# Weight sums of the first six matrices between the products of the matrix before, down sums one matrix later

## The chip, the core and the metric

One core of a Trainium2 chip runs the whole kernel. The metric is the device time of one execution in microseconds (us), lower being better. The engines named below are TensorE (PE in the profile, PEld for its weight loads), VectorE (DVE), ScalarE (ACT), GpSimd (POOL) and SyncE (SP), which issues nearly all DMAs here; each runs its own instructions in order and waits for the others by semaphores.

## What is computed

One layer of a hybrid encoder on 1024 tokens of width 1024 in float32: a half feed-forward block, a token mixer, a second half feed-forward block, each between two RMS norms with a shift, scale and gate worked out from a condition vector.

```python
def swiglu(u, w_gate, w_up, w_down):
    return (jax.nn.silu(u @ w_gate) * (u @ w_up)) @ w_down

def sublayer(h, i, fn, resid_w):
    shift, scale, gate = mod[:, i, 0, None, :], mod[:, i, 1, None, :], mod[:, i, 2, None, :]
    u = rms_norm(h, norm_pre[l, i]) * (1.0 + scale) + shift
    return h + resid_w * gate * rms_norm(fn(u), norm_post[l, i])

h = sublayer(h, 0, lambda u: swiglu(u, ffn1_w_gate[l], ffn1_w_up[l], ffn1_w_down[l]), 0.5)
h = sublayer(h, 1, lambda u: token_mixer(u, ...), 1.0)
h = sublayer(h, 2, lambda u: swiglu(u, ffn2_w_gate[l], ffn2_w_up[l], ffn2_w_down[l]), 0.5)
```

The hidden width of a feed-forward block is 2816. The change lies in the gate and up products of the two blocks; the mixer between them is not touched.

## The kernel before

**Arithmetic.** Every product of the feed-forward blocks is a 2x2 block product with seven block products in place of eight (a Strassen form), and every float32 operand is held as a high and a low half, so that one block product is 4 blocks x 3 matmuls = 12 matmuls of 128x512 (`product`, L291 to L299). The activations' block sums (T1 to T4, B22) are made once for each feed-forward block. The weights' block sums are made for each matrix: S1, S2, S3, S4.

**Matrices and pairs.** A chunk pair c (11 of them, `NPAIR`) has two matrices, gate and up; the names m0, m1 (pair 0), m2, m3 (pair 1), m4, m5 (pair 2) and so on are used below. A matrix is `start` (two products with A11 and A12), then `p6` (S2 x T2), `p5` (S1 x T1), `p7` (S3 x T3), `p3` (S4 x B22), `p4` (A22 x T4). For the first three pairs (`NFIRST`) all six `start`s run ahead, while the activations' second half is still being prepared; their raw weights are given up by then, and are loaded again for the sums (`again`).

**The steps that the change moves.** `sums` (L319) loads the four raw blocks of a matrix as two transfers of 512 KB, r1 (tag "raw", two buffers) and r2 (tag "raw2", two buffers), makes S2 and S1 with two VectorE operations (L330, L331) in a tile s21, casts that on ScalarE (L224) and subtracts on VectorE (L225) to get the halves, and makes S3 and S4 with two more VectorE operations (L334, L335) in a tile s34. `sums34` (L337) makes the halves of those, `last` (L341) the halves of A22, which are read from r2. `hidden` (L437) takes the four results of a finished pair, makes their block sums with four VectorE operations in two tiles, and stores five tiles to DRAM. `down_sums` (L462) loads the four raw blocks of one chunk of the down weights (tags "raw" and "raw2"), makes four sums on VectorE in two tiles (t21, t34) and stores these. The sum tiles of `sums`, `hidden` and `down_sums` all have the tag "s" with four buffers. `steps` is a generator that loads one 512 KB row block of the condition weights (wada) at a time and adds it up on VectorE (L89, L91).

**Order.** The kernel is written as a program in one order; a planner lays it out on the engines, taking of what is ready by its own reckoning the operation that stands first in the program. An operation later in the program can therefore run ahead of one that waits, but buffers of one tag are handed out in program order. In the program of before, m2's sums stand behind all of pair 0, its `hidden` and its `down_sums`; m4's sums stand behind all of pair 1 and its `hidden`:

```python
if c == 0:
    rest(late, mats[c], True)
else:
    for second, m in enumerate(mats[c] if c < NFIRST else pair(c)):
        if second:
            down_sums(fp, late, A[wd][c], c, hd)
        m.start()
        rest(late, [m], c < NFIRST)
hidden(late, c, mats[c][1].c, hd)
```

Of the kernel before, what the change touches and what calls it, by code (L numbers as in the profile page):

```python
# [33 lines left out]
NPAIR = NFF // 2  # L34
ROWS = 4
QT = 13
NFIRST = 3
# [9 lines left out]
def build(ctx, tc, A, out):  # L47
# [253 lines left out]
    class Matrix:  # L301
# [80 lines left out]
        def start(self):  # L382
            self.part(4)
# [27 lines left out]
        H, L = TB[n]  # L411
        return lambda k: (H[k], L[k])

    def rest(late, ms, again):

        if len(ms) == 2:
            for m in ms:
                m.p6()
            for m in ms:
                m.p5()  # L420
                m.p3()
                m.p7()
            for m in ms:
                m.last()
                m.p4()
            return
        m = ms[0]
        m.sums(late, again)
        m.sums34()
        m.last()  # L430
        m.p6()
        m.p5()
        m.p7()
        m.p3()
        m.p4()

    def hidden(late, c, hs, hd):  # L437


        a11, a12, a21, a22 = hs["C11"], hs["C21"], hs["C12"], hs["C22"]  # L440
        s21 = late.tile([P, 2, HALF], F32, name="s21", tag="s", bufs=4)
        s34 = late.tile([P, 2, HALF], F32, name="s34", tag="s", bufs=4)
        V.tensor_add(s21[:, 1], a21, a22)
        V.tensor_sub(s21[:, 0], s21[:, 1], a11)
        V.tensor_sub(s34[:, 0], a11, a21)
        V.tensor_sub(s34[:, 1], a12, s21[:, 0])
        for n, t in (("A11", a11), ("A12", a12), ("A22", a22)):
            hd[n, c] = dram.tile([P, HALF], F32, name=f"hd_{n}_{c}_{len(hd)}")
            store_queue(c).dma_start(hd[n, c], t)
        both(hd, "S2", "S1", c, s21)  # L450
        both(hd, "S3", "S4", c, s34)

    def store_queue(c):

        return POOL if c == NPAIR - 1 else SP

    def both(hd, n0, n1, c, t):
        d = dram.tile([P, 2, HALF], F32, name=f"d_{n0}_{c}")
        hd[n0, c], hd[n1, c] = d[:, 0], d[:, 1]
        store_queue(c).dma_start(d, t)  # L460

    def down_sums(fp, late, src, c, hd):  # L462

        r1 = wpool.tile([P, 2, HALF], F32, name="raw", tag="raw", bufs=2)
        SP.dma_start(r1, src[:, 0:2])
        r2 = fp.tile([P, 2, HALF], F32, name="raw2", tag="raw2", bufs=2)
        SP.dma_start(r2, src[:, 2:4])
        t21 = late.tile([P, 2, HALF], F32, name="t21", tag="s", bufs=4)
        t34 = late.tile([P, 2, HALF], F32, name="t34", tag="s", bufs=4)
        V.tensor_sub(t21[:, 1], r1[:, 1], r1[:, 0])  # L470
        V.tensor_sub(t21[:, 0], r2[:, 1], t21[:, 1])
        V.tensor_sub(t34[:, 0], r2[:, 1], r1[:, 1])
        V.tensor_sub(t34[:, 1], r2[:, 0], t21[:, 0])
        both(hd, "T2", "T1", c, t21)
        both(hd, "T3", "T4", c, t34)

    def ffn(wg, wu, wd, start, pending, steps_fn, per_pair, steps2_fn, i, res_src, dst):


        hd = {}  # L480

        with tc.tile_pool(name="ffa", bufs=1, side="left", reuse_waits="tile") as fp, \
                tc.tile_pool(name="ffa_ps", bufs=1, space=PSUM, reuse_waits="tile") as psum:
            mats = {}

            def pair(c):
                g = Matrix(fp, psum, A[wg][c], None)
                mats[c] = g, Matrix(fp, psum, A[wu][c], g)
                return mats[c]

            first = [m for c in range(NFIRST) for m in pair(c)]
            start(fp, psum, first)
            with tc.tile_pool(name="fft", bufs=1, side="left", reuse_waits="tile") as tp, ExitStack() as more:
                pools = [tp]
                later = pending(pools, fp, psum, tag="y")
                for n, m in enumerate(first):
                    m.start()
                    if n:
                        next(later)
                with tc.tile_pool(name="ffs", bufs=1, side="left", reuse_waits="tile") as sp:  # L500
                    for m in first[:2]:
                        m.sums(sp, True, "s0")
                    for m in first[:2]:
                        m.sums34()
                pools.append(more.enter_context(tc.tile_pool(name="fft2", bufs=1, side="left", reuse_waits="tile")))
                for _ in later:
                    pass
                yp.close()
                mod_tag[0] = "pa"
                with tc.tile_pool(name="late", bufs=1, side="right", reuse_waits="tile") as late:  # L510
                    steps = steps_fn(late, psum)
                    for c in range(NPAIR):
                        if c == 0:
                            rest(late, mats[c], True)
                        else:
                            for second, m in enumerate(mats[c] if c < NFIRST else pair(c)):
                                if second:
                                    down_sums(fp, late, A[wd][c], c, hd)
                                m.start()
                                rest(late, [m], c < NFIRST)  # L520
                        hidden(late, c, mats[c][1].c, hd)
                        if c == 0:
                            down_sums(fp, late, A[wd][c], c, hd)
                            continue
                        for _ in range(per_pair):
                            next(steps, None)
                    for _ in steps:
                        pass
# [3 lines left out]
        with tc.tile_pool(name="ffb0", bufs=1, side="left", reuse_waits="tile") as np_, \  # L532
# [4 lines left out]
            steps = steps2_fn(np_, psum)  # L537
# [171 lines left out]
    def no_steps(fp, psum):  # L709
        yield  # L710

    pending = ffn("wg1", "wu1", "wd1", start0, pending0, steps1, 3, steps1b, 0, lambda t: A["x"][t * P:(t + 1) * P, :], lambda t: h_dram[0][t])

    pending = mixer(locals())

    ffn("wg2", "wu2", "wd2", start_half, pending, lambda fp, psum: mod_gate(fp, psum, 2, 0.5), 1, no_steps, 2, lambda t: h_dram[1][t],
        lambda t: out[t * P:(t + 1) * P, :])
    yp.close()
# [581 lines left out]
```

## Time and profile before

| | us |
|---|---|
| runs (three), median | 2326.1 |
| lowest, highest | 2325.53, 2331.6 |
| the profiled execution, its own time | 2332.79 |
| its span from first to last instruction | 2331.0 |
| mean granted TensorE clock, share of full | 0.975 |

| engine | busy us | share of the span |
|---|---|---|
| TensorE matmuls | 2204.7 | 95% |
| VectorE | 1570.6 | 67% |
| ScalarE | 1047.5 | 45% |
| GpSimd | 70.0 | 3% |

The page's busy shares are means over stages with different limits, so they only say which engine to look at; where it waits is read from the timeline of that engine, and what ends its waits from the timelines of the engines that it waits for. A row of a timeline gives the start, the duration, the engine, the line, what is written and read, and in brackets the idle time of the engine before it with what ended it.

### The profile page before, as it was taken

The numbers are of one execution on the slowest core, as the hardware profiler recorded it, in microseconds if no ns is written. First come the engines' busy times: TensorE is split into PE (matmuls) and PEld (weight loads), VectorE is DVE, ScalarE is ACT, GpSimd is POOL, SyncE is SP. The second block draws the span as 40 slices with busy tenths as digits, with TensorE's granted clock in tenths as the row PEclk, the third lists the DMA queues.
The fourth block names the chain that finished last, engine by engine and source line by source line (L and its number), as shares of the span: only waits on it lengthen the run. The fifth ranks groups of instructions, "written<-read, shape, count | busy, mean of one in ns | idle before, by whom it ended". The sixth has DMA issues, their size and how long they took to land.

```text
span 2331.0 us, 28613 instructions
## 1 busy us (share of the span) xinstructions
PE 2204.7 (95%) x10420; PEld 1805.3 (77%) x10420; DVE 1570.6 (67%) x2612; ACT 1047.5 (45%) x1882; POOL 70.0 (3%) x90
## 2 busy tenths in 40 slices
PE   5989999989989989999999999999979999999998
PEld 3767788868868877878888888788767787877876
DVE  6885787566667587576677677665976666655565
ACT  4523333335445465454554455555723332325454
POOL 1000000000000010011001000000000000000000
PEclk8899999999999999999999999999989999999999
DMA  7283574358877211110111122764465443427667
GB/s 298 75 286 131 202 259 175 137 181 304 299 234 237 69 45 40 41 47 29 60 55 64 46 86 87 244 199 128 140 244 179 143 169 138 173 96 261 201 203 246
DMA packets 137678, 364.39 MB, mean 156 GB/s; under 512 B 16704, under 2 KB 20800, under 8 KB 137536
## 3 DMA queue, kind: packets, MB, share of 16 engines
q1 hardware_dynamic: 135904, 356.79, 45.0%
q0 software_dynamic: 1632, 5.77, 0.6%
q8 instruction: 81, 1.33, 0.2%
q14 instruction: 61, 0.50, 0.1%
HBM read 272.32 MB, written 90.18 MB: 156 GB/s over the span
## 4 chain that ended last, share of the span: by engine, by line
PE 67%; DVE 17%; DMA 8%; ACT 4%; issue 3%; SPq 0%; DVEq 0%; ACTq 0%
PE bank L299 9%; PE bank L297 9%; PE bank L298 9%; PE pps L765 4%; PE pps L763 4%; PE pps L767 4%; DMA stg<-in_wd 3%; DVE f L960 2%; PE bankA L547 2%; PE bankA L549 2%; PE bankA L548 2%; DMA stg<-d_T 2%; PE bankB L547 2%; PE bankB L548 2%; PE bankB L549 2%
## 5 line engine op out<-in xcount | busy, mean ns | idle before, releaser
L763 PE MATMUL pps<-uH,wsH 128*128 128x512 f32 x512 | 209.7, 410 | 0.0
L765 PE MATMUL pps<-uL,wsH 128*128 128x512 f32 x512 | 205.4, 401 | 0.0
L767 PE MATMUL pps<-uH,wsL 128*128 128x512 f32 x512 | 204.7, 400 | 0.0
L225 DVE TENSOR_TENSOR tbL<-stg,tbH 128x512 fp32r<-128x512 f32 x154 | 105.8, 689 | 113.7 <-ACT tbH L224 113.4
L224 ACT CAST tbH<-stg 128x512 fp32r<-128x512 f32 x154 | 95.6, 621 | 167.8 <-DMA stg<-d_T 98.6
L547 PE MATMUL bankA<-tbH,sbH 128*128 128x512 f32 x352 | 140.8, 402 | 18.3 <-ACT tbH L224 17.9
L297 PE MATMUL bank<-uH,wsH 128*128 128x512 f32 x352 | 141.4, 404 | 3.5 <-DVE uH L179 2.7
L298 PE MATMUL bank<-uL,wsH 128*128 128x512 f32 x352 | 140.3, 398 | 1.5 <-POOL uL L180 1.5
L548 PE MATMUL bankA<-tbL,sbH 128*128 128x512 f32 x352 | 140.4, 399 | 0.0
L549 PE MATMUL bankA<-tbH,sbL 128*128 128x512 f32 x352 | 139.6, 397 | 0.0
L299 PE MATMUL bank<-uH,wsL 128*128 128x512 f32 x352 | 139.2, 396 | 0.0
L224 ACT CAST wsH<-s 128x1024 fp32r<-128x1024 f32 x88 | 91.6, 1049 | 97.1 <-DVE s L331 88.0
L141 DVE TENSOR_TENSOR wsL<-raw,wsH 128x1024 fp32r<-128x1024 f32 x72 | 87.9, 1221 | 69.1 <-ACT wsH L140 67.5
L225 DVE TENSOR_TENSOR sbL<-stg,sbH 128x512 fp32r<-128x512 f32 (+1 forms) x176 | 108.8, 620 | 36.3 <-ACT sbH L224 34.6
L224 ACT CAST sbH<-stg 128x512 fp32r<-128x512 f32 (+1 forms) x176 | 98.9, 565 | 70.8 <-DMA stg<-hd_A 40.7
L364 ACT COPY q<-bank 128x512 f32<-128x512 f32 x44 | 25.8, 587 | 209.2 <-PE bank L299 209.2
L547 PE MATMUL bankB<-tbH,sbH 128*128 128x512 f32 x264 | 104.5, 396 | 11.3 <-ACT y L599 10.9
L767 PEld LDWEIGHTS pps<-uH,wsL 128*128 128x128 f32 x512 | 96.9, 189 | 17.9
L763 PEld LDWEIGHTS pps<-uH,wsH 128*128 128x128 f32 x512 | 97.6, 191 | 14.7
L225 DVE TENSOR_TENSOR wsL<-s,wsH 128x1024 fp32r<-128x1024 f32 x88 | 106.9, 1218 | 2.6 <-ACT wsH L224 2.0
L765 PEld LDWEIGHTS pps<-uL,wsH 128*128 128x128 f32 x512 | 97.2, 190 | 14.7
L548 PE MATMUL bankB<-tbL,sbH 128*128 128x512 f32 x264 | 104.2, 395 | 0.0
(247 smaller groups left out, 5947.7 us busy)
## 6 DMA issues: line engine op xcount, KB each, us to landing
wada<-in_wada SPq DMA_DIRECT2D x56, 512.0 KB, 5.6
raw<-in_wg SPq DMA_DIRECT2D x50, 512.0 KB, 6.7
raw<-in_wu SPq DMA_DIRECT2D x50, 512.0 KB, 4.4
raw<-in_wd SPq DMA_DIRECT2D x44, 512.0 KB, 4.5
stg<-hd_A SPq DMA_DIRECT2D x88, 256.0 KB, 4.3
stg<-d_S SPq DMA_DIRECT2D x88, 256.0 KB, 3.1
stg<-d_T SPq DMA_DIRECT2D x88, 256.0 KB, 3.5
d_S<-s SPq DMA_DIRECT2D x40, 512.0 KB, 2.7
```

Of the source, the lines that this page charges most:

```text
L141: eng.tensor_sub(l, raw, h.bitcast(F32))
L224: ACT.copy(h, src)
L225: V.tensor_sub(l, src, h.bitcast(F32))
L297: PE.matmul(ps, H[:, ks], bH, start=first and k == 0, stop=False, skip_group_check=not first)
L298: PE.matmul(ps, H[:, ks], bL, start=False, stop=False, skip_group_check=not first)
L299: PE.matmul(ps, L[:, ks], bH, start=False, stop=k == 3, skip_group_check=not first)
L547: PE.matmul(ps, sH[:, ts], tH, start=first, stop=False, skip_group_check=not check)
L548: PE.matmul(ps, sH[:, ts], tL, start=False, stop=False, skip_group_check=not check)
L549: PE.matmul(ps, sL[:, ts], tH, start=False, stop=last, skip_group_check=not check)
L763: PE.matmul(ps, aH, bH, start=i == 0, stop=False)
L765: PE.matmul(ps, aH, bL, start=False, stop=False)
L767: PE.matmul(ps, aL, bH, start=False, stop=i == n - 1)
```

## The change

The order of the program alone changes, for pairs 0, 1 and 2 of each of the two feed-forward blocks. The same loads, sums, casts, products and stores are made. A new function `rest_first` walks the six first matrices. The sums of m2 stand between the products p5 and p3 of m1, their halves of S3, S4 and A22 behind p4 of m1. From m2 on, each matrix has the sums of its successor between its p5 and p7, the halves of the successor's S3 and S4 between p3 and p4, and the successor's A22 behind p4. `last` of m0 and m1 moves ahead of their p3 and p7. `hidden` of a pair stands behind p6 of the next matrix. `down_sums` of pair 0 moves from behind pair 0 to behind p6 of m3, that of pair 1 from between m2 and m3 to behind p6 of m5, that of pair 2 from between m4 and m5 to behind pair 4. The `steps` of pairs 1 and 2 keep their number and are spread over the calls of `follow`. From pair 3 on the order is that of before, but for pair 2's down sums.

```diff
-    def rest(late, ms, again):
-
-        if len(ms) == 2:
-            for m in ms:
-                m.p6()
-            for m in ms:
-                m.p5()
-                m.p3()
-                m.p7()
-            for m in ms:
-                m.last()
-                m.p4()
-            return
-        m = ms[0]
-        m.sums(late, again)
+    def rest(late, m):
+
+        m.sums(late, False)
         m.sums34()
         m.last()
         m.p6()
...
+    def rest_first(late, ms, done):
+
+
+
+        for m in ms[:2]:
+            m.p6()
+        for i, m in enumerate(ms[:2]):
+            m.p5()
+            m.last()
+            if i:
+                ms[2].sums(late, True)
+            m.p3()
+            m.p7()
+        for m in ms[:2]:
+            m.p4()
+        ms[2].sums34()
+        ms[2].last()
+        for i in range(2, len(ms)):
+            m, nxt = ms[i], ms[i + 1] if i + 1 < len(ms) else None
+            m.p6()
+            done(i - 1)
+            m.p5()
+            if nxt is not None:
+                nxt.sums(late, True)
+            m.p7()
+            m.p3()
+            if nxt is not None:
+                nxt.sums34()
+            m.p4()
+            if nxt is not None:
+                nxt.last()
+        done(len(ms) - 1)
...
-                    for c in range(NPAIR):
-                        if c == 0:
-                            rest(late, mats[c], True)
-                        else:
-                            for second, m in enumerate(mats[c] if c < NFIRST else pair(c)):
-                                if second:
-                                    down_sums(fp, late, A[wd][c], c, hd)
-                                m.start()
-                                rest(late, [m], c < NFIRST)
+                    def follow(n):
+                        if n % 2:
+                            hidden(late, n // 2, mats[n // 2][1].c, hd)
+                        if n > 1:
+
+                            if n % 2 == 0:
+                                down_sums(fp, late, A[wd][n // 2 - 1], n // 2 - 1, hd)
+                            for _ in range(per_pair // 2 + (n % 2) * (per_pair % 2)):
+                                next(steps, None)
+
+                    rest_first(late, first, follow)
+                    for c in range(NFIRST, NPAIR):
+                        for second, m in enumerate(pair(c)):
+                            if second:
+                                down_sums(fp, late, A[wd][c], c, hd)
+                            m.start()
+                            rest(late, m)
                         hidden(late, c, mats[c][1].c, hd)
-                        if c == 0:
-                            down_sums(fp, late, A[wd][c], c, hd)
-                            continue
+                        if c == NFIRST + 1:
+                            down_sums(fp, late, A[wd][NFIRST - 1], NFIRST - 1, hd)
                         for _ in range(per_pair):
                             next(steps, None)
```

## Rows read from the trace of the kernel before

**Rows 1.** The page, part 1: busy time, share and instructions of each engine.

```profile
PE 2204.7 (95%) x10420; PEld 1805.3 (77%) x10420; DVE 1570.6 (67%) x2612; ACT 1047.5 (45%) x1882; POOL 70.0 (3%) x90
```

**Rows 2.** Timeline of TensorE: first matmuls of m2, m4, m6 (block 1), m2, m4 (block 2).

```profile
128.97 0.79 PE L297 MATMUL bank<-T2H,wsH 128*128 128x512 f32 x1 [6.13 <-ACT wsH L224]
...
163.25 0.79 PE L297 MATMUL bank<-T2H,wsH 128*128 128x512 f32 x1 [4.45 <-ACT wsH L224]
...
193.07 0.39 PE L297 MATMUL bank<-uH,wsH 128*128 128x512 f32 x1
...
1713.98 0.80 PE L297 MATMUL bank<-T2H,wsH 128*128 128x512 f32 x1 [9.40 <-ACT wsH L224]
...
1748.80 0.79 PE L297 MATMUL bank<-T2H,wsH 128*128 128x512 f32 x1 [4.17 <-ACT wsH L224]
```

**Rows 3.** Busy time by stretch: stretch, length, busy us of each engine, clock, DMA.

```profile
93.00:122.83 29.83, 29.83 (x135) 23.45 (x133) 25.60 (x40) 13.11 (x22) 0.00 (x0) 1.00 0.41 140
122.83:193.07 70.24, 59.55 (x241) 46.91 (x241) 49.60 (x67) 19.50 (x27) 0.00 (x0) 0.93 0.67 232
128.97:144.56 15.59, 15.59 (x60) 12.36 (x61) 13.63 (x19) 5.84 (x8) 0.00 (x0) 0.89 0.94 335
163.25:179.14 15.89, 15.78 (x61) 12.22 (x61) 12.10 (x17) 6.51 (x9) 0.00 (x0) 0.90 0.71 242
179.14:193.07 13.93, 13.93 (x61) 11.30 (x60) 5.12 (x7) 2.72 (x4) 0.00 (x0) 1.00 0.17 58
...
1704.58:1779.07 74.49, 60.92 (x242) 48.40 (x241) 45.86 (x65) 19.82 (x27) 0.00 (x0) 0.89 0.55 199
1704.58:1713.98 9.40, 0.01 (x1) 0.00 (x0) 8.12 (x14) 1.04 (x1) 0.00 (x0) 0.75 1.01 384
1713.98:1730.51 16.53, 16.52 (x60) 13.16 (x61) 12.25 (x17) 6.73 (x9) 0.00 (x0) 0.83 0.77 278
1748.80:1765.07 16.27, 16.27 (x61) 12.86 (x61) 12.10 (x17) 6.51 (x9) 0.00 (x0) 0.85 0.66 237
1765.07:1779.07 14.00, 14.00 (x62) 11.26 (x60) 5.14 (x7) 2.72 (x4) 0.00 (x0) 1.00 0.17 57
```

**Rows 4.** Timeline of VectorE: operations ahead of m2's sums, and L330 of m2.

```profile
115.67 0.69 DVE L403 TENSOR_TENSOR q<-bank,q 128x512 f32<-128x512 f32 x1 [3.88 <-PE bank L299]
...
124.76 0.68 DVE L473 TENSOR_TENSOR t<-raw,t 128x512 f32<-128x512 f32 x1
125.36 0.68 DVE L330 TENSOR_TENSOR s<-raw 128x512 f32<-128x512 f32 x1
...
1711.44 0.69 DVE L330 TENSOR_TENSOR s<-raw 128x512 f32<-128x512 f32 x1 [1.25 <-DMA d_S<-s]
1712.16 0.69 DVE L331 TENSOR_TENSOR s<-s,raw 128x512 f32<-128x512 f32 x1
```

**Rows 5.** Timeline of SP's DMA issues, and landing times of tile raw, 100 to 195.

```profile
110.58 0.33 SPq L467 DMA_DIRECT2D raw<-in_wd  x1
111.15 0.33 SPq L327 DMA_DIRECT2D raw<-in_wg  x1
111.57 1.46 SPq L87 DMA_DIRECT2D wada<-in_wada  x3
...
1686.27 0.33 SPq L467 DMA_DIRECT2D raw<-in_wd  x1
...
DMA to landing us min/median/max: 3.6/5.0/7.0
```

**Rows 6.** Busy time of a later stretch, pairs 5 and 6 of block 1.

```profile
271.52:349.00 77.48, 77.28 (x330) 61.58 (x329) 67.60 (x84) 26.30 (x36) 0.00 (x0) 1.00 0.77 268
```

**Rows 7.** Timeline of VectorE: L330 of m3 and m5 waiting for a load.

```profile
139.97 0.69 DVE L330 TENSOR_TENSOR s<-raw 128x512 f32<-128x512 f32 x1 [1.47 <-DMA raw<-in_wu]
...
1757.07 0.69 DVE L330 TENSOR_TENSOR s<-raw 128x512 f32<-128x512 f32 x1 [2.91 <-DMA raw<-in_wu]
```

**Rows 8.** Timeline of TensorE: the first matmul of block 1's down products.

```profile
517.64 0.80 PE L547 MATMUL bankA<-tbH,sbH 128*128 128x512 f32 x1 [5.72 <-ACT tbH L224]
```

## The prediction

> **What bounds the kernel now.** I read the page's busy shares first: TensorE is busy 95% of the span and VectorE 67% [rows 1]. A change of order can then only win where TensorE stands still, or runs at the low clock, in the stretch whose order is changed. So the timeline of TensorE over the first three pairs of each feed-forward block comes next. It shows four gaps, all ended by ScalarE's cast of S2 (L224): 6.13 us ahead of m2 and 4.45 ahead of m4 in block 1, 9.40 and 4.17 in block 2 [rows 2]. m3 and m5 have none. Then the busy times by stretch. m5 at the full clock takes 13.93 us in block 1 and 14.00 in block 2. [...]
>
> Why the cast is late is read on VectorE. In block 1 it sat idle for 3.88 us until a product of m1 (L403) came, then did the end of pair 0, and only behind the last of pair 0's down sums (L473, 124.76) came L330, the first of m2's sums, at 125.36, though m2's r2 was issued at 111.15 [rows 4, 5]. In block 2 the same L330 waited for `d_S<-s`, the store of pair 0's hidden sums [rows 4]: a buffer of tag "s" had to come free. With four buffers handed out in program order, `hidden` and `down_sums` of pair 0 hold all four, and m2's sums come behind the first store. They therefore can't start before pair 0's products are done, which is when TensorE needs their result.
>
> **The change part by part.** Terms are made against the profiled execution (2332.79 us in all, its span 2331.0).
>
> Sums of m2 and m4 ahead (the gain). From the end of p4 of m1 to the first matmul of m6, block 1 takes 70.24 us and block 2 74.49 [rows 3]. Four matrices at the full clock are 4 x 13.93 = 55.72 and 4 x 14.00 = 56.00. The excess is 14.5 and 18.5 us, 33.0 in all: 24.15 of gaps, 8.4 of slow matmuls behind them (1.66, 1.96, 2.53, 2.27), and 0.4 of rounding. 33 is the upper end.
>
> Whether m2's sums come in time. Now they are first in line for the "s" buffers, so the load of r2 decides. A slot of "raw2" came free in block 1 at 110.58 (the down weights took it) and in block 2 at 1686.27; a raw tile lands in 3.6 to 7.0 us [rows 5], so by 114.2 to 117.6. From the start of L330 to the first matmul it took 3.61 us in block 1 and 2.54 in block 2 [rows 2, 4]. Ready: 116.7 to 121.2, needed at 122.83: 1.6 to 6 us to spare. The idle 3.88 us of VectorE are where the work goes [rows 4]. In block 2, 1686.27 + 7.0 + 3.6 = 1696.9 against 1704.58. Moving `last` of m0 and m1 ahead can only bring the slot earlier; it puts one 0.69 us class operation ahead of L403, at nothing, since that idle time covers it.
>
> Whether m4's come in time. Their r2 needs a slot that the halves of m3's A22 give back, and these need the weight buffer that p3 of m2 frees, four products or 4 x 2.79 = 11.2 us after 122.83, so 134.0. With 3.6 us for the halves (an estimate: the whole chain of m2's sums above), 7.0 for landing and 3.6 for the sums it is 148.2, needed at 122.83 + 2 x 13.93 = 150.7. 2.5 us to spare at the worst. m3 and m5, ready a matrix ahead in the same way, have no less.
>
> Work on VectorE. Nothing is added. In block 1 the stretch from 93 to the start of m6 holds 25.60 + 49.60 us of it [rows 3]; one down sum (four operations 0.60 apart [rows 4], 2.4 us) leaves for behind pair 4. That is 72.8 us in 29.83 + 55.72 = 85.55, 85%. A later stretch had 67.60 us in 77.48, 87%, with TensorE busy 77.28 and no gap [rows 6]. So it fits. The down sum that lands behind pair 4 falls in stretches like that one, whose cover is the two `start` products per matrix; I cost it at nothing, and at its own 2.4 us per block if the cover is gone.
>
> DMAs. 70.24 us x 232 GB/s = 16.3 MB move in that stretch [rows 3]; a down sum's two loads and two stores of 0.52 MB leave it, 14.2 MB in 55.7 us, 255 GB/s. The later stretch had 268 GB/s at a share of 0.77 without a gap [rows 6]; the gap in block 2 had 384 [rows 3]. It fits on the mean. In SP's queue each load of `sums` now passes the stores of `hidden` and the two loads and two stores of `down_sums`; the latter come up to a matrix later, and nothing reads them before the down products. POOL's queue only carries stores of the last pair, which stay. The `steps` issue as many loads of wada and as many sums as before.
>
> Added waits. L330 of the successor now stands ahead of L398 of the running matrix on VectorE, and p4 waits for L398. L330 waited for its load 1.47 to 2.91 us in four places, m3 and m5 of both blocks [rows 7], and p3 gives 2.79 us of cover. So one such wait costs from nothing to about 2.9 us plus a slower clock of about 2 us. I take 3 us in all, one wait's worth over both blocks, since the loads have more time than before; ends 0 and 13.
>
> The end of phase one. The down products' first matmul waits 5.72 us for a cast of loaded data [rows 8]; it moves with the rest. A new layout of the program may shift it: 4 us either way, as an estimate below that one gap.
>
> Sum: 33 - 3 = 30 us off: 2332.79 becomes 2303, and the median, 6.7 us below the profiled execution, 2326.1 - 30 = 2296.
>
> **The rivals.** (a) Half back: the loads of m4 come late in both blocks, since loads of wada are issued in threes beside them [rows 5] and r2 has two slots that the down sums share. The gaps of m4 and their slow matmuls (4.45 + 1.96 and 4.17 + 2.27 = 12.9 us) stay: 2326.1 - 33 + 12.9 = 2306. For it: 2.5 us to spare at the worst. Against: that sum takes the longest landing. [...]
>
> (b) Slower: VectorE's queue blocks. L330 of the next matrix waits for r2 at the head of VectorE, L398 stands behind it, p4 waits, TensorE falls to the low clock. This can happen at the six matrices with a successor's sums in front (m2, m3 and m4 of each block). It outweighs the gain when each costs over 33 / 6 = 5.5 us; with 2 us of that the slow clock, the gap is 3.5 and the wait 3.5 + 2.79 = 6.3 us. At 7 us each, the longest landing [rows 5], it is 6 x (7.0 - 2.79 + 2) = 37 us against 33: 2330. Against: the longest wait of L330 seen is 2.91 [rows 7], and a load would have to be issued only when L330 is reached. [...]
>
> (c) No change: the planner lays the sums where they lay. It takes operations by readiness, so program order only ranks them: 2326, within 4 us. Against: L330 of m2 came just behind L473, as in the program, and its limit is the buffer order, which the program sets [rows 4].
>
> **How the numbers follow.** The forecast has 0.70 (2290 to 2303: residue 0 to 8 with the 4 us of the phase's end on the low side); (a) 0.17, (b) 0.05, (c) 0.08. The range of 8 in 10 reaches to (a) with the 4 us and 2 more of the runs' spread: 2288 to 2312. 0.3% (7 us) is about what a measurement of this kernel tells from no change. Faster by more: the forecast and (a), 0.87. Within: (c), 0.08. Slower: (b), 0.05.
>
> **What would show it.** Right: no gap ahead of m2 and m4, p4 of m1 to m6 in 56 to 59 us in both blocks with the granted clock at 1.00, L330 of m2 ahead of L403 and L398 of m1 on VectorE, and no wait for `d_S<-s`. (a) shows gaps ahead of m4 with L330 waiting for `raw<-in_wg`; (b) gaps ahead of T4 products, ended by L398; (c) the rows of before. The prediction is wrong if the gain is given back elsewhere, as a longer wait at the start of the down products or in the mixer, whose layout I take as unchanged.

## The result and the profile after

| | us |
|---|---|
| changed kernel, median of four runs | 2299.6 (2298.9 to 2301.9) |
| kernel before, median of four runs | 2327.8 (2325.5 to 2331.6) |
| ratio | 0.9872, 95% interval 0.9855 to 0.9889 |
| span of the profiled execution, before and after | 2331.0, 2297.1 |
| mean granted TensorE clock, before and after | 0.975, 0.984 |

The forecast was 2296 with a range of 2288 to 2312; 30 us off were forecast and 28 were measured. The page after has TensorE 12.7 us less busy than [rows 1], with the same number of matmuls: they took less time each. 8.6 of the 12.7 lie in the stretches of the first pairs below (59.55 and 60.92 us busy before [rows 3], 56.06 and 55.78 after), where they are the slow matmuls behind the gaps; the rest lies elsewhere.

```profile
PE 2192.0 (95%) x10420; PEld 1796.2 (78%) x10420; DVE 1569.5 (68%) x2612; ACT 1046.6 (46%) x1882; POOL 70.2 (3%) x90
```

Busy times by stretch of the kernel after (stretch, length, busy us of PE, PEld, DVE, ACT, POOL, clock, DMA share, GB/s). The first and the last row run from the end of p4 of m1 to the first matmul of m6, in block 1 and block 2, and answer to the 70.24 and 74.49 us of [rows 3]. The row between is m10 of block 1.

```profile
121.32:177.38 56.06, 56.06 (x242) 45.09 (x240) 43.73 (x59) 16.91 (x24) 0.00 (x0) 1.00 0.72 245
257.13:281.34 24.21, 21.62 (x87) 16.98 (x86) 20.33 (x30) 7.33 (x10) 0.00 (x0) 0.93 0.95 346
...
1690.60:1746.38 55.78, 55.78 (x241) 45.23 (x240) 41.39 (x57) 17.02 (x24) 0.00 (x0) 1.00 0.67 226
```

Both stretches of the first pairs are now without a gap and at the full clock: TensorE is busy for all of 56.06 and 55.78 us. That is 14.2 and 18.7 us less than before, 32.9 in all.

Timeline of TensorE of the kernel after: the first matmuls of m2 in block 1 (directly behind the last of m1, no idle time), then those of p6 of m10 in block 1 and in block 2. From m6 on a matrix begins with its `start`, so a gap "ahead of m10" stands between its `start` and its p6.

```profile
121.08 0.40 PE L299 MATMUL bank<-T4H,wsL 128*128 128x512 f32 x1
121.32 0.40 PE L297 MATMUL bank<-T2H,wsH 128*128 128x512 f32 x1
...
265.74 0.50 PE L297 MATMUL bank<-T2H,wsH 128*128 128x512 f32 x1 [2.58 <-ACT wsH L224]
266.07 0.59 PE L298 MATMUL bank<-T2L,wsH 128*128 128x512 f32 x1
266.46 0.63 PE L297 MATMUL bank<-T1H,wsH 128*128 128x512 f32 x1
...
1831.68 0.50 PE L297 MATMUL bank<-T2H,wsH 128*128 128x512 f32 x1 [1.25 <-ACT wsH L224]
1832.02 0.39 PE L298 MATMUL bank<-T2L,wsH 128*128 128x512 f32 x1
```

The gaps ahead of m10 are new; the kernel before has none there. m10 of block 1 takes 24.21 us where it took 20.20: 2.58 of the 4.01 are the gap, the other 1.43 the matmuls behind it, at first of 0.59 to 0.63 us in place of 0.39. Busy times by stretch of the kernel before: m6 to the first matmul of the down products in block 1, m10 of block 1, m6 to the down products in block 2.

```profile
193.07:517.64 324.57, 318.27 (x1381) 256.18 (x1379) 224.44 (x303) 109.23 (x149) 3.93 (x7) 1.00 0.53 183
272.83:293.03 20.20, 20.07 (x86) 15.90 (x85) 19.99 (x28) 9.34 (x12) 0.00 (x0) 1.00 0.89 313
...
1779.07:2103.35 324.28, 315.01 (x1349) 252.42 (x1348) 201.03 (x280) 104.74 (x146) 3.77 (x7) 0.99 0.43 152
```

And of the kernel after, m6 to the down products in block 1 and in block 2:

```profile
177.38:508.15 330.77, 320.41 (x1381) 256.96 (x1379) 226.93 (x307) 109.09 (x149) 3.93 (x7) 0.99 0.53 185
...
1746.38:2073.02 326.64, 315.36 (x1350) 252.27 (x1348) 203.83 (x284) 104.83 (x146) 3.77 (x7) 0.99 0.45 158
```

Block 1 went from 324.57 us to 330.77, block 2 from 324.28 to 326.64: 8.6 us given back.

The timeline of VectorE after shows both sides. In its first part L330 of m2 runs at 110.79, as soon as its load lands, ahead of the last product sums of m1 (L398 at 113.15); before, it ran at 125.36 [rows 4]. In the second part, eight matrices later, ahead of m10, pair 2's down sums (now L491 to L494) stand where m10's sums should start.

```profile
110.79 0.69 DVE L330 TENSOR_TENSOR s<-raw 128x512 f32<-128x512 f32 x1 [0.36 <-DMA raw<-in_wg]
...
113.15 0.69 DVE L398 TENSOR_TENSOR q<-bank,q 128x512 f32<-128x512 f32 x1 [0.47 <-PE bank L299]
...
257.08 0.68 DVE L491 TENSOR_TENSOR t<-raw 128x512 f32<-128x512 f32 x1
257.68 0.68 DVE L467 TENSOR_TENSOR s<-q,s 128x512 f32<-128x512 f32 x1
258.28 0.68 DVE L492 TENSOR_TENSOR t<-raw,t 128x512 f32<-128x512 f32 x1
258.89 0.68 DVE L493 TENSOR_TENSOR t<-raw,raw 128x512 f32<-128x512 f32 x1
259.49 0.68 DVE L494 TENSOR_TENSOR t<-raw,t 128x512 f32<-128x512 f32 x1
260.09 1.27 DVE L126 TENSOR_TENSOR grow<-gps,br 128x512 f32<-128x512 f32 x2
261.29 0.68 DVE L330 TENSOR_TENSOR s<-raw 128x512 f32<-128x512 f32 x1
```

### The profile page after: what moved, and what is told of

It is laid out like the page before. It is cut to its first block, busy times and chain, and to the rows that moved or that the text cites. A ratio compares the mean times of both kernels' runs of the same rounds, so it can differ in the third digit from the quotient of the medians.

```text
span 2297.1 us, 28628 instructions
## 1 busy us (share of the span) xinstructions
PE 2192.0 (95%) x10420; PEld 1796.2 (78%) x10420; DVE 1569.5 (68%) x2612; ACT 1046.6 (46%) x1882; POOL 70.2 (3%) x90
## 4 chain that ended last, share of the span: by engine, by line
PE 72%; DVE 15%; DMA 6%; ACT 4%; issue 2%; SPq 0%; DVEq 0%; ACTq 0%
PE bank L299 10%; PE bank L297 10%; PE bank L298 10%; PE pps L793 4%; PE pps L791 4%; PE pps L795 4%; PE bankA L575 3%; PE bankA L576 3%; PE bankA L577 3%; DVE f L988 2%; PE bankB L575 2%; PE bankB L576 2%; PE bankB L577 2%; DMA stg<-d_T 2%; PE vps L791 1%
## 5 line engine op out<-in xcount | busy, mean ns | idle before, releaser
L224 ACT CAST wsH<-raw 128x1024 fp32r<-128x1024 f32 (+1 forms) x88 | 73.2, 834 | 75.2 <-PE bank L298 47.4
```

The lines of the kernel that those rows point to most:

```text
L224: ACT.copy(h, src)
```

## The experiments

Two questions were open: why the sums were late before (buffers, or the rank in the program), and what gives back the 8.6 us. Kernels were compared by their ratio to the kernel before on the same chip; two chips were used, on which the kernel before had medians of 2333.2 and 2332.9 us. The changed kernel was run again among them.

**The changed kernel again.**

> The changed kernel again, beside the three others on the same chip. Expected 2300 us, 28 below the kernel before (range 24 to 33). If the 33.9 us between the two profiled executions were the true size, it would be 34 below; the medians of the first runs say 28.

Ratio 0.9885 (0.9866 to 0.9904): 2304.8 against 2333.2, 28 us. Its profile repeats the pattern: 55.77 and 56.00 us for the two stretches, 332.27 and 325.77 from m6 to the down products.

**The kernel before, profiled again.**

> The kernel before, profiled once more on this chip, to see how far its gaps vary: 6.1, 4.5, 9.4 and 4.2 us ahead of m2 and m4 in the first profile. Theory: they come from the order of the program, so each is there again within 2 us. If a gap differs by more, the profile of one execution overstates or understates what the change takes away.

Timeline of TensorE of that execution, the first matmuls of m2 and m4 in both blocks:

```profile
129.34 0.80 PE L297 MATMUL bank<-T2H,wsH 128*128 128x512 f32 x1 [6.13 <-ACT wsH L224]
...
164.59 0.79 PE L297 MATMUL bank<-T2H,wsH 128*128 128x512 f32 x1 [4.32 <-ACT wsH L224]
...
1717.28 0.79 PE L297 MATMUL bank<-T2H,wsH 128*128 128x512 f32 x1 [9.20 <-ACT wsH L224]
...
1752.14 0.80 PE L297 MATMUL bank<-T2H,wsH 128*128 128x512 f32 x1 [4.18 <-ACT wsH L224]
```

All four are there within 0.2 us of [rows 2], so they belong to the kernel and not to one execution. With the changed kernel's second profile the stretches of the first pairs give 34.2 us, and from m6 to the down products 8.7 are lost: 25.5 net of the 28.5 between these two spans. Of the 33.9 us between the first two profiles 24.3 are explained in this way. The other 9.6 lie outside these stretches: 1.5 us ahead of the first, 4.5 between block 1's down products and block 2's m2, 3.6 behind the last. In the second pair of profiles the same places give 0.5, 2.7 and -0.2, so they are not a steady part of the gain.

**Two tags, the program order of before.**

```diff
-            s21 = late.tile([P, 2, HALF], F32, name="s21", tag=tag, bufs=4)
-            self.s34 = s34 = late.tile([P, 2, HALF], F32, name="s34", tag=tag, bufs=4)
+            s21 = late.tile([P, 2, HALF], F32, name="s21", tag=tag, bufs=2 if tag == "s" else 4)
+            self.s34 = s34 = late.tile([P, 2, HALF], F32, name="s34", tag=tag, bufs=2 if tag == "s" else 4)
...
-        s21 = late.tile([P, 2, HALF], F32, name="s21", tag="s", bufs=4)
-        s34 = late.tile([P, 2, HALF], F32, name="s34", tag="s", bufs=4)
+        s21 = late.tile([P, 2, HALF], F32, name="s21", tag="h", bufs=2)
+        s34 = late.tile([P, 2, HALF], F32, name="s34", tag="h", bufs=2)
...
-        t21 = late.tile([P, 2, HALF], F32, name="t21", tag="s", bufs=4)
-        t34 = late.tile([P, 2, HALF], F32, name="t34", tag="s", bufs=4)
+        t21 = late.tile([P, 2, HALF], F32, name="t21", tag="h", bufs=2)
+        t34 = late.tile([P, 2, HALF], F32, name="t34", tag="h", bufs=2)
```

> The program order of before, untouched; the sum tiles of sums keep the tag s with two buffers, those of hidden and down_sums get a tag of their own with two buffers, so the memory is the same. Theory of the buffers (the hand-out of the s buffers in program order held the sums back): L330 of m2 and m4 runs before hidden of the pair ahead, the four gaps go, and the time is that of the changed kernel or a little better, as pair 2's down sums stay at their place: 2292 to 2300. Rival (the rank in the program held them back): the gaps of 6.1, 4.5, 9.4 and 4.2 us stay and the time is that of before within 4 us.

Ratio 0.9941 (0.9918 to 0.9964), 13 us below before: neither of the two. Timeline of TensorE of this kernel, m2 and m3 of block 1, then m3 of block 2:

```profile
122.16 0.39 PE L297 MATMUL bank<-T2H,wsH 128*128 128x512 f32 x1
...
144.49 0.79 PE L297 MATMUL bank<-T2H,wsH 128*128 128x512 f32 x1 [8.18 <-ACT wsH L224]
...
1728.43 0.80 PE L297 MATMUL bank<-T2H,wsH 128*128 128x512 f32 x1 [13.05 <-ACT wsH L224]
```

And on the timeline of VectorE of the same kernel, L330 of m3 in block 2:

```profile
1725.35 0.69 DVE L330 TENSOR_TENSOR s<-raw 128x512 f32<-128x512 f32 x1 [7.83 <-DMA raw<-in_wu]
```

The gaps ahead of m2 and m4 are gone with no line of the program moved. For m2 it was therefore the buffers of tag "s"; for m4 this kernel alone doesn't show it, as its m4 was needed later, behind the new wait of m3 (the kernel with two tags and later down sums below settles it). In the place of the old gaps m3 has a gap in each block, of 8.18 and 13.05 us, and it is ended by its load: L330 waited 7.83 us with VectorE idle until r2 (raw, from in_wu) landed. SP issued r2 of m3 in block 1 at the same time in both kernels, first the kernel before, then the one with two tags:

```profile
135.52 0.33 SPq L327 DMA_DIRECT2D raw<-in_wu  x1
```

```profile
135.57 0.42 SPq L327 DMA_DIRECT2D raw<-in_wu  x1
```

The load of m3 had been that late before too: two pairs' down sums stand ahead of it for the slots of "raw" and "raw2". The gap ahead of m2 had hidden it, since m3 was needed that much later. The changed kernel issues it at 109.79. SP's DMA issues of the kernel after, r2 of m2 and of m3 in block 1:

```profile
106.82 0.33 SPq L327 DMA_DIRECT2D raw<-in_wg  x1
...
109.79 0.33 SPq L327 DMA_DIRECT2D raw<-in_wu  x1
```

**The down sums' half of the change alone** (sums and tags as before; the down sums behind p6 of m3, behind p6 of m5 and behind pair 4).

```diff
-    def rest(late, ms, again):
+    def rest(late, ms, again, between=None):
...
         m.p6()
+        if between is not None:
+            between()
...
-                                if second:
+                                if second and c >= NFIRST:
                                     down_sums(fp, late, A[wd][c], c, hd)
                                 m.start()
-                                rest(late, [m], c < NFIRST)
+                                rest(late, [m], c < NFIRST, (lambda: down_sums(fp, late, A[wd][c - 1], c - 1, hd))
+                                     if second and c < NFIRST else None)
...
                         if c == 0:
-                            down_sums(fp, late, A[wd][c], c, hd)
                             continue
+                        if c == NFIRST + 1:
+                            down_sums(fp, late, A[wd][NFIRST - 1], NFIRST - 1, hd)
```

> Only the down sums' half of the change: one tag s as before, the sums as before, the down sums of pairs 0, 1 and 2 where the change puts them. Theory of the buffers: m2's sums still stand behind hidden of pair 0, but four VectorE operations (2.4 us) and the wait for a store fall away, so m2's gap shrinks to 2 to 4 us and m4's of 4.5 and 4.2 us stay; the loss ahead of m10 (6.2 and 2.4 us in the changed kernel) comes in: 0 to 10 us below before. Rival (the down sums' place is what counts, as they delay the loads): all four gaps go, 25 us or more below.

Ratio 0.9988 (0.9977 to 0.9998), 3 us. Timeline of TensorE of this kernel, m2, m4 and m10 of block 1, then of block 2:

```profile
125.42 0.67 PE L297 MATMUL bank<-T2H,wsH 128*128 128x512 f32 x1 [2.53 <-ACT wsH L224]
...
160.13 0.79 PE L297 MATMUL bank<-T2H,wsH 128*128 128x512 f32 x1 [5.00 <-ACT wsH L224]
...
277.86 0.50 PE L297 MATMUL bank<-T2H,wsH 128*128 128x512 f32 x1 [2.58 <-ACT wsH L224]
...
1714.22 0.80 PE L297 MATMUL bank<-T2H,wsH 128*128 128x512 f32 x1 [4.33 <-ACT wsH L224]
...
1749.00 0.80 PE L297 MATMUL bank<-T2H,wsH 128*128 128x512 f32 x1 [4.17 <-ACT wsH L224]
...
1864.46 0.50 PE L297 MATMUL bank<-T2H,wsH 128*128 128x512 f32 x1 [1.25 <-ACT wsH L224]
```

m2's gap shrank by 3.6 and 5.1 us (from 6.13 and 9.40, [rows 2]), m4's stayed, and the gaps ahead of m10 came in with the very sizes of the changed kernel, 2.58 and 1.25. So the loss comes from the down sums' half.

**The sums' half of the change alone** (`follow` keeps the down sums of pair 0 behind `hidden` of pair 0, those of pairs 1 and 2 behind p6 of m3 and m5; nothing behind pair 4).

```diff
+                        if n in (1, 2, 4):
+                            down_sums(fp, late, A[wd][n // 2], n // 2, hd)
...
-                            if n % 2 == 0:
-                                down_sums(fp, late, A[wd][n // 2 - 1], n // 2 - 1, hd)
...
-                        if c == NFIRST + 1:
-                            down_sums(fp, late, A[wd][NFIRST - 1], NFIRST - 1, hd)
```

> Only the sums' half of the change: the sums between the products of the matrix ahead, the down sums of pair 0 behind hidden of pair 0, those of pair 1 and 2 behind p6 of m3 and m5. Theory of the buffers (load slots): m2 has no gap; the down sums take a raw2 slot ahead of m3, so a gap of 5 to 13 us comes ahead of m3, as in the kernel with two tags alone, and the whole is 10 to 20 us below before. Rival (the place of the sums is enough): no gap, and as pair 4 has no second down sum, 30 to 36 us below before.

Ratio 0.9858 (0.9842 to 0.9874), 35 us: the rival held. I had expected a gap ahead of m3 for want of a load slot. Busy times by stretch of this kernel, p4 of m1 to m6, then m6 to the down products, in block 1:

```profile
123.03:179.34 56.31, 56.04 (x242) 45.15 (x241) 46.01 (x63) 17.29 (x24) 0.00 (x0) 1.00 0.82 282
179.34:504.10 324.76, 318.17 (x1381) 256.21 (x1380) 224.16 (x303) 109.04 (x149) 3.93 (x7) 0.99 0.53 182
```

Here only pair 0's down sums stand ahead of m3's loads, not two pairs', and r2 of m3 goes out at 122.12:

```profile
122.12 0.33 SPq L327 DMA_DIRECT2D raw<-in_wu  x1
```

That is early enough. From m6 on the blocks are as long as before (block 2: 324.40), without the 8.6 us that the changed kernel loses there. So the sums' half carries the whole gain, and the later places that the change gives to the down sums add nothing to it.

**Pair 2's down sums at another place.** In the changed kernel they go between p5 and p7 of m9, where VectorE had 5.84 us idle. Timeline of VectorE of the changed kernel, the sum behind p7 of m9:

```profile
250.48 0.69 DVE L398 TENSOR_TENSOR q<-bank,q 128x512 f32<-128x512 f32 x1 [5.84 <-PE bank L299]
```

```diff
-    def rest(late, m):
+    def rest(late, m, between=None):
...
         m.p6()
         m.p5()
+        if between is not None:
+            between()
...
-                            rest(late, m)
+                            rest(late, m, (lambda: down_sums(fp, late, A[wd][NFIRST - 1], NFIRST - 1, hd))
+                                 if second and c == NFIRST + 1 else None)
...
-                        if c == NFIRST + 1:
-                            down_sums(fp, late, A[wd][NFIRST - 1], NFIRST - 1, hd)
```

> The changed kernel with pair 2's down sums between p5 and p7 of m9 in place of behind pair 4. In the changed kernel block 1 loses 6.2 us and block 2 2.4 us between m6 and the down products against before, with gaps of 2.58 and 1.25 us ahead of m10. Theory A (the four down sum operations stand on VectorE between hidden of pair 4 and m10's sums): the gaps of m10 go, 5 to 8 us off the changed kernel, 2292 to 2295. Theory B (the loss comes from other traffic on the DMA queues, loads of wada above all, which the move shifts): gaps somewhere between m10 and m13 remain, less than 3 us off, 2297 or more.

Ratio 0.9860 (0.9840 to 0.9879), 2299.7 us (2298.0 to 2300.0) against 2304.8 (2300.9 to 2311.4) of the changed kernel beside it: 5 us off. Busy times by stretch of this kernel, m6 to the down products in both blocks:

```profile
179.46:504.05 324.59, 318.38 (x1382) 256.20 (x1380) 226.76 (x307) 109.12 (x149) 3.92 (x7) 1.00 0.54 188
...
1748.09:2073.43 325.34, 315.07 (x1350) 252.53 (x1348) 203.43 (x284) 104.81 (x146) 3.77 (x7) 0.99 0.46 158
```

Block 1 is at 324.59, as before the change (324.57); neither block has a gap ahead of m10. Theory A holds for block 1. In block 2 the gap is gone too, and 1.1 us against before stay.

**Two tags and the down sums later, the sums in the program order of before** (the edits of the kernel with two tags and of the one with the down sums' half put together).

> The order of the sums as in the kernel before (all of a matrix' sums stand behind its predecessor's products and behind hidden), with two edits: hidden and down_sums have a tag of their own for their sum tiles, two buffers each, and the down sums of pairs 0, 1 and 2 stand where the change puts them (behind p6 of m3, behind p6 of m5, behind pair 4). Theory of the buffers (tag s held up m2 and m4, the load slots raw and raw2 handed to the down sums first held up m3 in the kernel with two tags alone): no gap ahead of m2 to m5, 28 to 36 us below before. Rival (the sums must stand between the products of the matrix ahead): gaps of 3 us or more remain among m2 to m5, at most 20 below before.

Ratio 0.9838 (0.9824 to 0.9853), 39 us below before, and the buffer theory's forecast even exceeded. Busy times by stretch of this kernel: p4 of m1 to m6 and m6 to the down products in block 1, then in block 2.

```profile
123.00:178.77 55.77, 55.77 (x241) 45.21 (x240) 49.22 (x65) 19.16 (x26) 0.00 (x0) 1.00 0.81 271
178.77:501.88 323.11, 316.83 (x1382) 256.52 (x1380) 225.01 (x302) 107.59 (x147) 3.93 (x7) 0.99 0.55 189
1684.41:1741.63 57.22, 56.62 (x242) 44.89 (x240) 44.81 (x61) 19.01 (x26) 0.00 (x0) 1.00 0.73 239
1741.63:2063.83 322.20, 313.01 (x1350) 252.86 (x1348) 203.75 (x279) 103.13 (x143) 3.77 (x7) 0.99 0.47 158
```

The first pairs run without a gap ahead of any matrix though every `sums` stands behind its predecessor's products in the program, and those of m2 and m4 behind `hidden` as well (0.6 us of waits ahead of two p4 are left in block 2). And pair 2's down sums stand behind pair 4, with the same loads and stores as in the changed kernel, but m10 has no gap: its sums no longer queue for a buffer behind them. Timeline of VectorE of this kernel, L330 of m10 in block 1 and the first operation of `hidden` of pair 4:

```profile
242.53 0.69 DVE L330 TENSOR_TENSOR s<-raw 128x512 f32<-128x512 f32 x1 [4.03 <-DMA raw<-in_wg]
...
256.46 0.68 DVE L445 TENSOR_TENSOR s<-q 128x512 f32<-128x512 f32 x1
```

This kernel differs from the one with the down sums' half alone in nothing but the tags. There the gaps ahead of m2, m4 and m10 were 2.53, 5.00 and 2.58 us in block 1 and 4.33, 4.17 and 1.25 in block 2; here none of the six is left. So the shared buffers made the gaps of m2, of m4 and of m10, and theory B (DMA traffic) isn't needed for the last.

**Both edits on the changed kernel** (two tags, pair 2's down sums in m9).

> The changed kernel with both edits: two tags and pair 2's down sums in m9. If the gaps of pairs 1 and 2 are gone already in the changed kernel, two tags can't bring more there; with theory A it is as fast as the kernel with the down sums in m9 alone, 2291 to 2295. If two tags bring more than 2 us beyond that, buffers of s also held up later pairs.

Ratio 0.9837 (0.9818 to 0.9857), 2294.0 us, 5.7 below the kernel with the down sums in m9 alone. From m6 to the down products its blocks take 322.88 and 322.78 us against 324.59 and 325.34, and the kernel above had 323.11 and 322.20: the common tag also held up the later pairs a little. This kernel and the one above are the two fastest here, and can't be told apart.

## Why the prediction was right, point by point

**What bound the kernel.** Right. The two stretches gave 32.9 us of the 33.0 that were worked out from the gaps and the slow matmuls behind them, and the clock in them is 1.00. Before, each of the four gaps cost twice: its idle time, and behind it m2 and m4 took 1.66 to 2.53 us longer than m5, at mean clocks of 0.83 to 0.90 [rows 3]. The matmuls directly behind the gap took 0.63 us in place of 0.39. Timeline of TensorE of the kernel before, m2 of block 1:

```profile
129.56 0.63 PE L298 MATMUL bank<-T2L,wsH 128*128 128x512 f32 x1
...
132.43 0.39 PE L298 MATMUL bank<-T2L,wsH 128*128 128x512 f32 x1
```

**The cause.** Right, and shown: with the down sums at their new place and the sums in the order of before, a tag of its own for the sum tiles takes away the gaps ahead of m2 and m4. The order of the program is one way to get a buffer in time; what it sets is the hand-out of buffers.

**Whether m2's and m4's sums come in time.** Right. r2 of m2 went out at 106.82 (I used 110.58) and L330 ran at 110.79, ten microseconds ahead of need. m4 had no gap either; its L330 ran at 137.51, for a need at about 149. Timeline of VectorE after, L330 of m4 in block 1:

```profile
137.51 0.69 DVE L330 TENSOR_TENSOR s<-raw 128x512 f32<-128x512 f32 x1 [1.03 <-DMA raw<-in_wg]
```

**The added waits (3 us).** Wrong place. L330 of a successor never held up p4 in the first pairs of the changed kernel. (I counted six matrices with a successor's sums in front; with m1, which has m2's, there are eight.) The mechanism of rival (b) showed once, in m13 of block 1, with another load. Timeline of VectorE after, then of TensorE after:

```profile
337.52 1.28 DVE L91 SCALAR_TENSOR_TENSOR macc<-wada,csil,macc 128x1024 f32<-128x1024 f32 x1 [2.17 <-DMA wada<-in_wada]
338.73 0.68 DVE L398 TENSOR_TENSOR q<-bank,q 128x512 f32<-128x512 f32 x1
```

```profile
335.16 0.39 PE L299 MATMUL bank<-T3H,wsL 128*128 128x512 f32 x1
...
339.46 0.50 PE L297 MATMUL bank<-T4H,wsH 128*128 128x512 f32 x1 [1.10 <-DVE q L398]
```

L91 stood 2.17 us at the head of VectorE for a load of wada, L398 stood behind it, and p4 came 1.10 us late (1.92 in the second profile): one place, where 3 us had been set aside for all. L398 reads the result of p7, whose last matmul (the first row of TensorE here) ended at 335.55; L398 started at 338.73, as L91 ended.

**The down sum behind pair 4 (costed at nothing).** This is the step that failed. I named the two `start` products as its cover and 2.4 us per block as its price without one. In block 1 it cost 6.2 us, in block 2 2.4; the kernel with these sums in m9 has neither gap. My cover was that of an average stretch, [rows 6] with 87% on VectorE. But at the turn of a pair VectorE does `hidden` and the successor's sums in one run, and in block 1 the gate's rows (L126, L127) as well: there was no idle time to take four more operations. The four operations stood between `hidden` and L330 of m10 for the same reason as pair 0's did before the change: tag "s" in program order. In block 1 the 2.4 became 6.2: 4.0 in m10 (the gap of 2.58 and 1.43 of slow matmuls) and gaps of 0.40, 0.39, 1.10 and 0.33 us in m12 to m14. I had found the ring of buffers at m2 and not looked for it at the new place.

**Rival (a), m4's loads late.** Didn't come: L330 of m4 waited 1.03 and 2.04 us for its load in the two blocks, early enough not to hold up TensorE. In block 1 SP issued its r2 at 131.65, ahead of the next loads of wada at 134.37, so a load of m4 behind loads of wada was not seen there. **Rival (c), no change.** Its premise, that the rank only orders, was right for the sums, but the buffers follow the program.

**The end of phase one (4 us either way).** It hardly moved: the wait ahead of the down products is 5.27 us in block 1 in place of 5.72, and 9.42 in block 2 in place of 8.71.

**Why 28 and not 33.** 32.9 gained less 8.6 given back is 24.3 by the first pair of profiles and 25.5 by the second; the medians say 28. The 3 to 4 us between are not settled: they are within what differs between executions in untouched parts. The forecast's 30 came close with one term too high (3 us of waits that didn't come) and one too low (8.6 us of the down sum, put at nothing), and it is luck that these and the unsettled part nearly cancel; the gain of 33 itself was no luck.

## What to carry to other kernels

Where buffers of one tag are handed out in program order, read a late start as a question of who holds the buffer before moving any code: here a tag of its own for the work on the critical path gave 39 us with the down sums moved, and only 13 without; the new order of the sums gave 35 by itself, and 28 with the down sum behind pair 4. A removed gap uncovers the next late load, as m3's here, so ask of every wait behind it how early it would be needed then. Work moved off the path must be costed against the busy time at its new place, not against the mean of the stage.

## What was not expected of the hardware

A gap of 2.58 us ahead of m10 in block 1 was followed by matmuls of 0.59 to 0.63 us (granted clock 0.93 over m10), a gap of 1.25 us in block 2 by matmuls of 0.39 to 0.50 (granted clock 1.00): the first lost 1.43 us more behind the gap, the second 0.33 in the same way (m10 of block 2 took 21.32 us where it took 19.74). In m13 of the changed kernel's second profile matmuls of 0.63 us followed a gap of 1.92 as well. The gaps of one program came back within 0.2 us in another execution, while the untouched parts of two executions of the changed kernel differ by 5.8 us in sum.
